# Splitting the first FFN products off r1 for one and a half feature tiles, and all squares for r2 on GpSimd

## The chip, the cores and the metric

The kernel runs on one core of a Trainium2 chip. The metric is the device time of one execution in microseconds (us), lower is better; it is given as the median of several runs. The engines are TensorE (PE, its weight loads are PEld), VectorE (DVE), ScalarE (ACT), GpSimd (POOL) and SyncE (SP), whose queue issues the weight loads.

## The reference

One layer of a streaming encoder, on 256 prompt rows and 64 sample rows (T = 320 columns in the kernel, which works on transposed data), model width 2048, feed-forward width 5632, all in float32:

```python
def layer(x, ...):
    h = rmsnorm(x, g_mix_pre)
    z = h @ w_in                      # pooling input u, and q, k, v
    ...                               # causal pooling mixer; chunk-banded attention with sinks
    mix = concat(pool_out, attn_out) @ w_out
    x = x + rmsnorm(mix, g_mix_post)              # r1 is the factor of this norm
    h = rmsnorm(x, g_ffn_pre)                     # r2 the factor of this one
    f = (silu(h @ w_gate) * (h @ w_up)) @ w_down
    return x + rmsnorm(f, g_ffn_post), ...
```

`rmsnorm(x, g)` is x times g divided by the root of the mean square over the 2048 features.

## The kernel before

The 2048 features lie in 16 tiles of 128 partitions (KT = 16), each with 320 columns. Every float32 matrix product is made of three matmuls on rounded halves: weights and data are split into a rounded part ("hi") and the rest ("lo"), and hi x hi, hi x lo and lo x hi are added in PSUM. ScalarE makes the hi part, VectorE the lo part (`lo` of a weight chunk, line 62; `scaled_split`, lines 120 to 122, for data). `chunk` loads 128x1024 weights into one of six raw buffers (two pools of three taken in turn) and splits them; hi and lo have three buffers each.

The change lies between the output projection and the first feed-forward products. There, `mix` holds the projection scaled by its gain and `x2` the input. r1 needs the sum of all squares of the projection, so it comes late. `rstd` (lines 103 to 118) sums squares over the partitions with a ones-matmul, and takes logarithm and exponential on ScalarE and four steps on VectorE.

The first four products (gate and up of the first two output tiles, 512 columns of weights in `wgu`) don't wait for r1 with all of their features. For the first AHEAD = 2 feature tiles, x2 and mix are multiplied by the weights apart: x2's products go into the four PSUM tiles `gu`, mix's into the four `qd`, from `pf`, which holds the split halves of both. They need no r1; `qd` is multiplied by r1 afterwards (`qr`, lines 622 and 625) and added to `gu` (line 627). These are 48 matmuls.

The residual loop (lines 559 to 573) goes over the feature tiles in the order 2 to 15, 0, 1. I call the place in that order the step n. For each step, `residual` makes t = mix x r1 on VectorE and adds it to x2, on VectorE for the first two steps and for even tiles, on GpSimd for odd tiles; it is called LEAD = 2 steps ahead. Then `scaled_split` writes the two halves of h2, ScalarE squares x2 into mix (line 568), and for the 14 tiles of the loop that weren't taken ahead twelve matmuls add to `gu`. Behind the loop, 14 squares are summed on GpSimd (line 577); the 15th tile's square and that sum go into two ones-matmuls for r2 (line 629). `gate_up(0)` and `gate_up(1)`, the next four products, run meanwhile; the first of them is `acc_g` at line 176.

Each engine executes its instructions in order. The order is made by a scheduler that places instructions by their dependencies, so it isn't always that of the code; `issue_after(ins)` ties the instructions in its block behind `ins`, if they are on the same engine as `ins`.

Of the kernel before, what the change touches and what calls it, by code (L numbers as in the profile page):

```python
# [12 lines left out]
F32R = mybir.dt.float32r  # L13
AF = mybir.ActivationFunctionType
ALU = mybir.AluOpType
# [6 lines left out]
P = 128  # L22
D = 2048
KT = D // P
NPR = 256
NSA = 64
T = NPR + NSA
# [5 lines left out]
NFF = FF // P  # L33
NH = NFF // 2
EPS = 1e-6
AHEAD = 2
LEAD = 2
WINS = (2, 4, 8, 16)


# [5 lines left out]
def trunk_kernel(ctx, tc, xT, wkv, wi, wo, wgu, wg, wu, wd, pw, par, ckT, cv, spT, yT, okT, ovT, ocv, ou):  # L46
    nc = tc.nc
# [19 lines left out]
    def chunk(src, kc, name, eng=nc.scalar):  # L67

        w = src.shape[2]
        n = kc * w  # L70
        pool, tag, bufs = raws[next(turn) % len(raws)]
        raw = pool.tile([P, 1024], F32, tag=tag, name=f"raw_{name}", bufs=bufs)
        nc.sync.dma_start(raw[:, :n].rearrange("p (k w) -> p k w", k=kc), src)
        hi, lo = split(raw, n, name, eng)
        return (hi[:, :n].rearrange("p (k w) -> p k w", k=kc),
                lo[:, :n].rearrange("p (k w) -> p k w", k=kc))
# [54 lines left out]
    def h1s(k):  # L131
        return h1[k // 4][:, 0, k % 4, :], h1[k // 4][:, 1, k % 4, :]
# [4 lines left out]
    for k0, n in ((0, 1), (1, 1)) + tuple((k, 2) for k in range(2, KT, 2)):  # L137
# [10 lines left out]
        wh, wl = chunk(wkv[:, k0 : k0 + n, :], n, f"kv{k0}", eng=nc.vector if k0 == 0 else nc.scalar)  # L148
        for k in range(k0, k0 + n):
            hh, hl = h1s(k)  # L150
            nc.vector.scalar_tensor_tensor(hl, x[:, k, :], col(C_PRE, k), hh.bitcast(F32),
                                           op0=ALU.mult, op1=ALU.subtract)
            for i, (ws, xs) in enumerate(((wh, hh), (wh, hl), (wl, hh))):
                for m in range(4):
                    nc.tensor.matmul(kv[m][:, :T], ws[:, k - k0, m * P : (m + 1) * P], xs,
                                     start=k == 0 and i == 0, stop=k == KT - 1 and i == 2)
# [108 lines left out]
    ks = at.tile([P, 2, T], F32, name="ks", tag="PT")  # L265
# [17 lines left out]
    for w in range(-1, 5):  # L283
        n = P if w < 4 else CH
# [190 lines left out]
    n = 3  # L475
# [23 lines left out]
    mix = big.tile([P, KT, T], F32, tag="C", name="mix")  # L499
# [17 lines left out]
    for m0 in range(0, KT, 2):  # L517
        between = ([*unit(11)[0], st_mm(1)], [st_mm(0)]) if m0 == 0 else ()

        def evac(i, a, m0=m0):  # L520
            m = m0 + i
            sq_acc(m, a[:, :T], acc1, "mix")
            nc.scalar.activation(mix[:, m, :], a[:, :T], AF.Copy, scale=col(C_POST, m))
        gemm([(wout(m), f"o{m}") for m in (m0, m0 + 1)], Ms, evac, between=between)
        if m0 == 0:
            actx.close()
            fctx = ctx.enter_context(tc.tile_pool(name="ff", bufs=1))
            raws += [(fctx, "wraw2", 3)]
        if m0 == 2:

            pf = fctx.tile([P, 2, 2, AHEAD, T], F32R, tag="A4", name="pf")
            for i, src in enumerate((x2, mix)):
                for k in range(AHEAD):
                    scaled_split(pf[:, i, 0, k, :], pf[:, i, 1, k, :], src[:, k, :], col(C_FPRE, k))
    ahead = chunk(wgu[:, 0:AHEAD, :], AHEAD, "gu0")
    r1 = rstd([acc1, last_sq.pop()], "1")


# [1 line left out]
    gu = [bank("ga"[m // 2], f"gu_{m}") for m in range(4)]  # L540
    qd = [bank("agga"[m], f"qd_{m}") for m in range(4)]
    wh, wl = ahead
    for i, accs in enumerate((gu, qd)):
        for m in range(4):
            sl = slice(m * P, m * P + P)
            for k in range(AHEAD):
                mm3(accs[m][:, :T], wh[:, k, sl], wl[:, k, sl], pf[:, i, 0, k, :], pf[:, i, 1, k, :],
                    k == 0, i == 1 and k == AHEAD - 1)
    qr = fctx.tile([P, 4, T], F32, tag="A5", name="qr")
    order = (*range(AHEAD, KT), *range(AHEAD))  # L550

    def residual(n):
        k = order[n]
        t = tmp320(f"t_{k}")
        nc.vector.tensor_tensor(t, mix[:, k, :], r1, op=ALU.mult)
        eng = nc.vector if n < 2 or k % 2 == 0 else nc.gpsimd
        return eng.tensor_tensor(x2[:, k, :], x2[:, k, :], t, op=ALU.add)

    for n in range(LEAD):
        residual(n)  # L560
    for n, k in enumerate(order):
        if n + LEAD < KT:
            added = residual(n + LEAD)
        if k >= AHEAD and k % 2 == 0:
            wh, wl = chunk(wgu[:, k : k + 2, :], 2, f"gu{k}")
        hh, hl = h2[k // 4][:, 0, k % 4, :], h2[k // 4][:, 1, k % 4, :]
        scaled_split(hh, hl, x2[:, k, :], col(C_FPRE, k))
        nc.scalar.activation(mix[:, k, :], x2[:, k, :], AF.Square)
        if k >= AHEAD:
            for i, (ws, xs) in enumerate(((wh, hh), (wl, hh), (wh, hl))):  # L570
                for m in range(4):
                    nc.tensor.matmul(gu[m][:, :T], ws[:, k % 2, m * P : m * P + P], xs, start=False,
                                     stop=i == 2 and k == KT - 1)

    with tc.issue_after(added.ins):
        for k in order[1:-1]:
            nc.gpsimd.tensor_tensor(mix[:, AHEAD, :], mix[:, AHEAD, :], mix[:, k, :], op=ALU.add)

    def h2s(k):
        return h2[k // 4][:, 0, k % 4, :], h2[k // 4][:, 1, k % 4, :]  # L580
# [8 lines left out]
    r2 = last_sig = None  # L589
    for half in range(2):  # L590
        s = [big.tile([P, 2, 4, T], F32R, tag=f"A{i}", name=f"s{half}_{i}") for i in range(4)]
        s += [fctx.tile([P, 2, 4, T], F32R, tag="A4", name=f"s{half}_4"),
              fctx.tile([P, 2, 2, T], F32R, tag="A5", name=f"s{half}_5")]

        def ss(k):
            return s[k // 4][:, 0, k % 4, :], s[k // 4][:, 1, k % 4, :]

        def evac_gu(n, ag, au):
            nm = f"{half}_{n}"
            g = tmp320(f"g_{nm}", "ev")  # L600
            uu = fctx.tile([P, T], F32, tag="ev2", name=f"u_{nm}", bufs=2)
            for i, (o, acc) in enumerate(((g, ag), (uu, au))):
                nc.vector.tensor_tensor(o, acc[:, :T], r2, op=ALU.mult)  # L603
            sg = fctx.tile([P, T], F32, tag="sg", name=f"sg_{nm}", bufs=2)
            nonlocal last_sig
            last_sig = nc.scalar.activation(sg, g, AF.Sigmoid)
            nc.gpsimd.tensor_tensor(g, g, uu, op=ALU.mult)  # L607
            nc.vector.tensor_tensor(g, g, sg, op=ALU.mult)
            sh, sl = ss(n)
            nc.scalar.copy(sh, g)  # L610
            nc.vector.tensor_tensor(sl, g, sh.bitcast(F32), op=ALU.subtract)

        def gate_up(b, lo_last=False):
            held = []
            gemm([(wgs(b), f"g{b}"), (wus(b), f"u{b}")], h2s, lambda i, a: held.append(a), tag="ga", lo_last=lo_last)
            return held

        n0 = 0
        if half == 0:

            for m in range(2):
                nc.vector.tensor_tensor(qr[:, m, :], qd[m][:, :T], r1, op=ALU.mult)
            held = gate_up(0, lo_last=True)
            for m in range(2, 4):
                nc.vector.tensor_tensor(qr[:, m, :], qd[m][:, :T], r1, op=ALU.mult)
            for m in range(4):
                nc.vector.tensor_tensor(qr[:, m, :], gu[m][:, :T], qr[:, m, :], op=ALU.add)
            held += gate_up(1)
            r2 = rstd([mix[:, order[-1], :], mix[:, AHEAD, :]], "2")
            evac_gu(0, qr[:, 0, :], qr[:, 1, :])  # L630
            evac_gu(1, qr[:, 2, :], qr[:, 3, :])
            evac_gu(2, *held[:2])
            evac_gu(3, *held[2:])
            n0 = 4
            f = big.tile([P, KT, T], F32, tag="C", name="f")
        for n in range(n0, NH):
            evac_gu(n, *gate_up(half * NH + n - 2))

        if half:
            with tc.issue_after(last_sig.ins):  # L640
                nc.scalar.preload_act_table_set(LNEXP)
        for m in range(KT):
            def evac(_, a, m=m):
                if m == KT - 1:
                    if half:
                        sq_acc(m, a[:, :T], acc3, "f")
                        nc.scalar.activation(f[:, m, :], a[:, :T], AF.Copy, scale=col(C_FPOST, m))
                elif half == 0:
                    nc.scalar.copy(f[:, m, :], a[:, :T])
                else:  # L650
                    nc.vector.tensor_tensor(f[:, m, :], f[:, m, :], a[:, :T], op=ALU.add)
                    sq_acc(m, f[:, m, :], acc3, "f")
                    nc.scalar.activation(f[:, m, :], f[:, m, :], AF.Copy, scale=col(C_FPOST, m))
            if m == KT - 1 and half == 0:
                held = bank("g", "acc_last")
            gemm([((lambda c, l, m=m: wd[half, m, :, c : c + l, :]), f"d{half}_{m}")], ss, evac, kt=NH,
                 tag="ag"[m % 2], accs=[held] if m == KT - 1 else None,
                 first=half == 0 or m < KT - 1, last=half == 1 or m < KT - 1)
# [8 lines left out]
    for k, n, how in TAIL:  # L667
# [7 lines left out]
        else:  # L675
            eng = nc.gpsimd if how == "g" else nc.vector
# [79 lines left out]
```

## Time and profile before

| | us |
|---|---|
| median of 3 runs | 1254.17 (1253.84 to 1254.76) |
| profiled execution | 1253.9 |
| its span, first to last instruction | 1252.1 |
| TensorE busy | 1238.6 (99%) |
| VectorE busy | 665.8 (53%) |
| ScalarE busy | 504.8 (40%) |
| GpSimd busy | 170.6 (14%) |

The rows come from the profiled execution; times in them are us from the start of its span, durations of one instruction in groups are ns. A row of the time list shows the start, the length, the engine, the line, the operation with the tile it writes and those it reads, the shape and the count of merged instructions, and in brackets how long the engine sat idle before it and what ended that. Instructions of an engine overlap at their ends, so the distance from one start to the next is what an instruction costs in a full queue. A released matmul is recorded with its full passage through the array, so its length is more than the distance to the next.

### The profile page before, as it was taken

Reading aid. Unit: us, or ns where it says so; the run is one execution under the profiler, and the core shown is the slowest. Engines: PE = TensorE matmul, PEld = TensorE weight load, DVE = VectorE, ACT = ScalarE, POOL = GpSimd, SP = SyncE. Lnnn points to the kernel's source line nnn. Section 1 sums busy time; section 2 is a strip of 40 time slices with the busy share of each in tenths; the row PEclk is TensorE's granted clock in tenths of the full one; section 3 lists DMA queues with packets and bytes.
Section 4 is the critical chain, followed back from the end, with each engine's and each line's share of the span. In section 5 each row is a group of like instructions: output and inputs, shape, how many; then the busy total and the mean of one; then the engine's idle time right before and its main releaser. Section 6 shows DMA issues by size and latency. Waiting matters only on the chain.

```text
span 1252.1 us, 20398 instructions
## 1 busy us (share of the span) xinstructions
PE 1238.6 (99%) x8404; PEld 1229.8 (98%) x8404; DVE 665.8 (53%) x889; ACT 504.8 (40%) x770; POOL 170.6 (14%) x153
## 2 busy tenths in 40 slices
PE   8999999999999999999999999999999999999997
PEld 8999999999999999999999999999999999999995
DVE  8867874336965455554433333554555455443435
ACT  5655654345543333333333333333333333443432
POOL 8202211122721000000000000000000000011112
PEclk9999999999999999999999999999999999999998
DMA  6654347443444444444455554444444444445532
GB/s 237 186 178 123 123 152 256 150 152 119 151 141 161 152 147 148 146 153 150 142 149 148 148 156 162 142 152 151 151 152 152 152 151 138 146 144 156 150 93 84
DMA packets 64125, 189.22 MB, mean 151 GB/s; under 512 B 15264, under 2 KB 16928, under 8 KB 64032
## 3 DMA queue, kind: packets, MB, share of 16 engines
q1 hardware_dynamic: 60480, 187.19, 46.1%
q8 instruction: 66, 1.08, 0.4%
q10 hardware_dynamic: 3552, 0.72, 0.3%
q14 instruction: 27, 0.22, 0.1%
HBM read 182.98 MB, written 3.27 MB: 149 GB/s over the span
## 4 chain that ended last, share of the span: by engine, by line
PE 93%; DVE 4%; issue 1%; DMA 1%; ACT 0%; POOL 0%; SPq 0%; DVEq 0%; ACTq 0%
PE acc_u L80 9%; PE acc_u L79 9%; PE acc_u L81 9%; PE acc_g L80 8%; PE acc_g L79 8%; PE acc_g L81 8%; PE acc_d L79 8%; PE acc_d L81 8%; PE acc_d L80 8%; PE acc_o L79 3%; PE acc_o L81 3%; PE acc_o L80 3%; PE acc_q L79 2%; PE acc_q L81 1%; PE acc_q L80 1%
## 5 line engine op out<-in xcount | busy, mean ns | idle before, releaser
L79 PE MATMUL acc_u<-h,hi_u 128*128 128x320 f32 x792 | 245.4, 310 | 0.0
L81 PE MATMUL acc_u<-h,lo_u 128*128 128x320 f32 x792 | 244.7, 309 | 0.0
L80 PE MATMUL acc_u<-h,hi_u 128*128 128x320 f32 x792 | 244.7, 309 | 0.0
L79 PE MATMUL acc_g<-h,hi_g 128*128 128x320 f32 x664 | 205.4, 309 | 0.0
L81 PE MATMUL acc_g<-h,lo_g 128*128 128x320 f32 x664 | 205.2, 309 | 0.0
L80 PE MATMUL acc_g<-h,hi_g 128*128 128x320 f32 x664 | 205.2, 309 | 0.0
L79 PE MATMUL acc_d<-s,hi_d 128*128 128x320 f32 x660 | 203.9, 309 | 0.0
L80 PE MATMUL acc_d<-s,hi_d 128*128 128x320 f32 x660 | 203.9, 309 | 0.0
L81 PE MATMUL acc_d<-s,lo_d 128*128 128x320 f32 x660 | 203.9, 309 | 0.0
L62 DVE TENSOR_TENSOR lo_d<-raw_d,hi_d 128x1024 fp32r<-128x1024 f32 (+1 forms) x96 | 110.3, 1149 | 175.6 <-ACT hi_d L60 175.6
L62 DVE TENSOR_TENSOR lo_g<-raw_g,hi_g 128x1024 fp32r<-128x1024 f32 x84 | 119.4, 1422 | 111.6 <-ACT hi_g L60 111.5
L60 ACT CAST hi_d<-raw_d 128x1024 fp32r<-128x1024 f32 (+1 forms) x96 | 93.8, 977 | 192.1 <-PE acc_d L80 179.3
L60 ACT CAST hi_g<-raw_g 128x1024 fp32r<-128x1024 f32 x84 | 88.3, 1051 | 180.7 <-PE acc_u L80 94.1
L60 ACT CAST hi_u<-raw_u 128x1024 fp32r<-128x1024 f32 x100 | 105.1, 1051 | 128.6 <-PE acc_g L80 102.9
L62 DVE TENSOR_TENSOR lo_u<-raw_u,hi_u 128x1024 fp32r<-128x1024 f32 x100 | 124.9, 1249 | 47.7 <-ACT hi_u L60 47.4
L79 PEld LDWEIGHTS acc_u<-h,hi_u 128*128 128x128 f32 x792 | 148.7, 188 | 0.0
L81 PEld LDWEIGHTS acc_u<-h,lo_u 128*128 128x128 f32 x792 | 148.7, 188 | 0.0
L80 PEld LDWEIGHTS acc_u<-h,hi_u 128*128 128x128 f32 x792 | 148.6, 188 | 0.0
L607 POOL TENSOR_TENSOR g<-g,u 128x320 f32<-128x320 f32 x44 | 41.5, 945 | 688.9 <-DVE u L603 665.6
L80 PEld LDWEIGHTS acc_g<-h,hi_g 128*128 128x128 f32 x664 | 124.7, 188 | 0.1
L79 PEld LDWEIGHTS acc_g<-h,hi_g 128*128 128x128 f32 x664 | 124.6, 188 | 0.1
L81 PEld LDWEIGHTS acc_g<-h,lo_g 128*128 128x128 f32 x664 | 124.6, 188 | 0.0
(210 smaller groups left out, 2018.1 us busy)
## 6 DMA issues: line engine op xcount, KB each, us to landing
raw_g<-wg SPq DMA_DIRECT2D x84, 512.0 KB, 3.6
raw_u<-wu SPq DMA_DIRECT2D x84, 512.0 KB, 3.6
raw_d<-wd SPq DMA_DIRECT2D x64, 512.0 KB, 3.5
raw_o<-wo SPq DMA_DIRECT2D x32, 512.0 KB, 3.8
raw_d<-wd SPq DMA_DIRECT2D x32, 384.0 KB, 3.4
raw_q<-wi SPq DMA_DIRECT2D x16, 512.0 KB, 3.9
raw_u<-wi SPq DMA_DIRECT2D x16, 512.0 KB, 3.7
raw_gu<-wgu SPq DMA_DIRECT2D x8, 512.0 KB, 3.5
```

The lines of the kernel that those rows point to most:

```text
L60: (eng.copy if eng is nc.scalar else eng.tensor_copy)(hi[:, :n], raw[:, :n])
L62: nc.vector.tensor_tensor(lo[:, :n], raw[:, :n], hi.bitcast(F32)[:, :n], op=ALU.subtract)
L79: nc.tensor.matmul(out, wh, xh, start=start, stop=False)
L80: nc.tensor.matmul(out, wh, xl, start=False, stop=False)
L81: nc.tensor.matmul(out, wl, xh, start=False, stop=stop)
L607: nc.gpsimd.tensor_tensor(g, g, uu, op=ALU.mult)
```

## The change

AHEAD becomes a pair. Feature tile 0 is still taken ahead in all four products, tile 1 only in the first two; its part of products 2 and 3 comes in the residual loop, with a weight chunk of its own (128x256). The order of the loop is now 2, 3, 4, 1, 5 to 15, 0. GpSimd makes the residual adds of the even steps from step 2 on, in place of those of the odd tiles; the last add, of step 15, is on VectorE. In the code, the first step's residual stands alone ahead of the loop, and the second's behind it. All 15 remaining squares are added into tile 2's on GpSimd, so that r2 needs one ones-matmul.

```diff
-AHEAD = 2
-LEAD = 2
+AHEAD = (4, 2)
+ORDER = (2, 3, 4, 1, *range(5, 16), 0)
...
-            for k in range(AHEAD):
+            n = sum(m < a for a in AHEAD)
+            for k in range(n):
                 mm3(accs[m][:, :T], wh[:, k, sl], wl[:, k, sl], pf[:, i, 0, k, :], pf[:, i, 1, k, :],
-                    k == 0, i == 1 and k == AHEAD - 1)
+                    k == 0, i == 1 and k == n - 1)
     qr = fctx.tile([P, 4, T], F32, tag="A5", name="qr")
-    order = (*range(AHEAD, KT), *range(AHEAD))
 
     def residual(n):
-        k = order[n]
+        k = ORDER[n]
         t = tmp320(f"t_{k}")
         nc.vector.tensor_tensor(t, mix[:, k, :], r1, op=ALU.mult)
-        eng = nc.vector if n < 2 or k % 2 == 0 else nc.gpsimd
+        eng = nc.vector if n < 2 or n % 2 else nc.gpsimd
         return eng.tensor_tensor(x2[:, k, :], x2[:, k, :], t, op=ALU.add)
 
-    for n in range(LEAD):
-        residual(n)
-    for n, k in enumerate(order):
-        if n + LEAD < KT:
-            added = residual(n + LEAD)
-        if k >= AHEAD and k % 2 == 0:
+    residual(0)
+    for n, k in enumerate(ORDER):
+        if n == 0:
+            residual(1)
+        if n + 2 < KT:
+            added = residual(n + 2)
+        m0 = AHEAD[k] if k < len(AHEAD) else 0
+        if m0 == 0 and k % 2 == 0:
             wh, wl = chunk(wgu[:, k : k + 2, :], 2, f"gu{k}")
+        ws, ks = (wh, wl), k % 2
+        if 0 < m0 < 4:
+            ws, ks = chunk(wgu[:, k : k + 1, m0 * P : 4 * P], 1, f"gu_{k}"), 0
...
-        if k >= AHEAD:
-            for i, (ws, xs) in enumerate(((wh, hh), (wl, hh), (wh, hl))):
-                for m in range(4):
-                    nc.tensor.matmul(gu[m][:, :T], ws[:, k % 2, m * P : m * P + P], xs, start=False,
-                                     stop=i == 2 and k == KT - 1)
+        for i, (w, xs) in enumerate(((ws[0], hh), (ws[1], hh), (ws[0], hl))):
+            for m in range(m0, 4):
+                o = (m - (m0 if 0 < m0 < 4 else 0)) * P
+                nc.tensor.matmul(gu[m][:, :T], w[:, ks, o : o + P], xs, start=False, stop=i == 2 and k == KT - 1)
 
     with tc.issue_after(added.ins):
-        for k in order[1:-1]:
-            nc.gpsimd.tensor_tensor(mix[:, AHEAD, :], mix[:, AHEAD, :], mix[:, k, :], op=ALU.add)
+        for k in ORDER[1:]:
+            nc.gpsimd.tensor_tensor(mix[:, ORDER[0], :], mix[:, ORDER[0], :], mix[:, k, :], op=ALU.add)
...
-            r2 = rstd([mix[:, order[-1], :], mix[:, AHEAD, :]], "2")
+            r2 = rstd([mix[:, ORDER[0], :]], "2")
```

GpSimd's queue from the last sum for r1 on, before the change (the number at the end of a `t` tile's name apart, the first number is the feature tile: `t_5` is tile 5's product with r1):

```order
L515 TENSOR_TENSOR acc1_2265<-acc1_2265,sq_mix_14_3357 128x320
L557 TENSOR_TENSOR x2_2259<-x2_2259,t_5_3473 128x320
L557 TENSOR_TENSOR x2_2259<-x2_2259,t_7_3515 128x320
L557 TENSOR_TENSOR x2_2259<-x2_2259,t_9_3557 128x320
L557 TENSOR_TENSOR x2_2259<-x2_2259,t_11_3599 128x320
L557 TENSOR_TENSOR x2_2259<-x2_2259,t_13_3641 128x320
L557 TENSOR_TENSOR x2_2259<-x2_2259,t_15_3683 128x320
L557 TENSOR_TENSOR x2_2259<-x2_2259,t_1_3725 128x320
L577 TENSOR_TENSOR mix_2264<-mix_2264 128x320 x14
```

All seven residual adds stand ahead of the 14 sums of squares. The same queue after the change:

```order
L515 TENSOR_TENSOR acc1_2265<-acc1_2265,sq_mix_14_3357 128x320
L557 TENSOR_TENSOR x2_2259<-x2_2259,t_4_3437 128x320
L581 TENSOR_TENSOR mix_2264<-mix_2264 128x320 x2
L557 TENSOR_TENSOR x2_2259<-x2_2259,t_5_3479 128x320
L581 TENSOR_TENSOR mix_2264<-mix_2264 128x320 x2
L557 TENSOR_TENSOR x2_2259<-x2_2259,t_7_3521 128x320
L581 TENSOR_TENSOR mix_2264<-mix_2264 128x320 x2
L557 TENSOR_TENSOR x2_2259<-x2_2259,t_9_3563 128x320
```

The adds and the sums now alternate, one add and two sums, and go on so up to the add of tile 15, behind which three sums stand.

VectorE's queue at the end of the residual loop, before the change (`h2_3` holds the halves of tiles 12 to 15, `h2_0` those of tiles 0 to 3):

```order
L62 TENSOR_TENSOR lo_gu14_3708<-raw_gu14_3704,hi_gu14_3706 128x1024
L557 TENSOR_TENSOR x2_2259<-x2_2259,t_0_3701 128x320
L122 SCALAR_TENSOR_TENSOR h2_3_3385<-x2_2259,pr_71,h2_3_3385 128x320
L555 TENSOR_TENSOR t_1_3725<-mix_2264,r_1_3380 128x320
L122 SCALAR_TENSOR_TENSOR h2_3_3385<-x2_2259,pr_71,h2_3_3385 128x320
L122 SCALAR_TENSOR_TENSOR h2_0_3382<-x2_2259,pr_71,h2_0_3382 128x320
L622 TENSOR_TENSOR qr_3442<-qd_0_3390,r_1_3380 128x320
L622 TENSOR_TENSOR qr_3442<-qd_1_3391,r_1_3380 128x320
L122 SCALAR_TENSOR_TENSOR h2_0_3382<-x2_2259,pr_71,h2_0_3382 128x320
L62 TENSOR_TENSOR lo_g0_0_3778<-raw_g0_0_3774,hi_g0_0_3776 128x1024
```

The split of tile 1 is the `h2_0` row behind the two `qr`. After the change:

```order
L62 TENSOR_TENSOR lo_gu14_3714<-raw_gu14_3710,hi_gu14_3712 128x1024
L557 TENSOR_TENSOR x2_2259<-x2_2259,t_0_3707 128x320
L122 SCALAR_TENSOR_TENSOR h2_3_3385<-x2_2259,pr_71,h2_3_3385 128x320 x2
L122 SCALAR_TENSOR_TENSOR h2_0_3382<-x2_2259,pr_71,h2_0_3382 128x320
L626 TENSOR_TENSOR qr_3430<-qd_0_3390,r_1_3380 128x320
L626 TENSOR_TENSOR qr_3430<-qd_1_3391,r_1_3380 128x320
L62 TENSOR_TENSOR lo_g0_0_3779<-raw_g0_0_3775,hi_g0_0_3777 128x1024
```

All splits, tile 1's at step 3 among them, now stand ahead of `qr`.

## Rows read from the trace of the kernel before

**Rows 1.** The page's first part: busy us, share of the span, instructions of each engine.

```profile
PE 1238.6 (99%) x8404; PEld 1229.8 (98%) x8404; DVE 665.8 (53%) x889; ACT 504.8 (40%) x770; POOL 170.6 (14%) x153
```

**Rows 2.** Stretches: from:to, length, busy us of PE, PEld, DVE, ACT, POOL; clock, DMA.

```profile
10.00:20.00 10.00, 7.93 (x51) 7.41 (x52) 10.00 (x7) 6.63 (x12) 9.94 (x9) 1.00 0.68 238
...
305.00:330.00 25.00, 24.75 (x168) 24.26 (x166) 24.92 (x40) 17.61 (x35) 13.36 (x9) 1.00 0.31 106
330.00:345.00 15.00, 15.00 (x103) 15.00 (x103) 11.94 (x13) 5.51 (x6) 14.22 (x11) 1.00 0.59 187
...
1240.00:1252.00 12.00, 6.33 (x12) 3.87 (x12) 7.90 (x9) 2.56 (x6) 3.42 (x2) 0.64 0.55 205
```

**Rows 3.** Time list, TensorE, at the loop's start and behind its end.

```profile
304.65 0.75 PE L572 MATMUL gu<-h,hi_gu 128*128 128x320 f32 x4
305.24 0.75 PE L572 MATMUL gu<-h,lo_gu 128*128 128x320 f32 x4
...
329.96 2.58 PE L176 MATMUL acc_g<-h,hi_g 128*128 128x320 f32 x16 [0.23 <-DVE qr L622]
```

**Rows 4.** Time list, VectorE, from r1 to the loop's end.

```profile
301.50 0.90 DVE L555 TENSOR_TENSOR t<-mix,r 128x320 f32<-128x320 f32 x2
302.31 0.89 DVE L557 TENSOR_TENSOR x<-x,t 128x320 f32<-128x320 f32 x2
303.11 0.48 DVE L555 TENSOR_TENSOR t<-mix,r 128x320 f32<-128x320 f32 x1
303.52 0.55 DVE L122 SCALAR_TENSOR_TENSOR h<-x,pr,h 128x320 fp32r<-128x320 f32 x1
303.98 0.48 DVE L557 TENSOR_TENSOR x<-x,t 128x320 f32<-128x320 f32 x1
...
308.01 1.17 DVE L555 TENSOR_TENSOR t<-mix,r 128x320 f32<-128x320 f32 x1
309.11 1.21 DVE L62 TENSOR_TENSOR lo_gu<-raw_gu,hi_gu 128x1024 fp32r<-128x1024 f32 x1
310.24 0.48 DVE L557 TENSOR_TENSOR x<-x,t 128x320 f32<-128x320 f32 x1
...
328.94 0.88 DVE L622 TENSOR_TENSOR qr<-qd,r 128x320 f32<-128x320 f32 x2
329.74 0.54 DVE L122 SCALAR_TENSOR_TENSOR h<-x,pr,h 128x320 fp32r<-128x320 f32 x1
```

**Rows 5.** Groups by shape, VectorE, 300 to 330 us: count, busy us, mean ns.

```profile
L122 DVE SCALAR_TENSOR_TENSOR h<-x,pr,h 128x320 fp32r<-128x320 f32 x16 | 11.1, 699 | 0.0
L555 DVE TENSOR_TENSOR t<-mix,r 128x320 f32<-128x320 f32 x16 | 9.7, 611 | 0.0
```

**Rows 6.** Time list, GpSimd: two residual adds and the sums of squares.

```profile
307.71 1.13 POOL L557 TENSOR_TENSOR x<-x,t 128x320 f32<-128x320 f32 x1 [1.24 <-DVE t L555]
311.67 3.06 POOL L557 TENSOR_TENSOR x<-x,t 128x320 f32<-128x320 f32 x1 [2.83 <-DVE t L555]
...
328.63 20.03 POOL L577 TENSOR_TENSOR mix<-mix 128x320 f32<-128x320 f32 x14
```

**Rows 7.** Time list at the kernel's head, VectorE, then GpSimd.

```profile
30.41 1.63 DVE L62 TENSOR_TENSOR lo_kv<-raw_kv,hi_kv 128x1024 fp32r<-128x1024 f32 x1
...
34.24 1.62 DVE L62 TENSOR_TENSOR lo_kv<-raw_kv,hi_kv 128x1024 fp32r<-128x1024 f32 x1
...
29.99 0.97 POOL L145 TENSOR_TENSOR sqx<-x 128x320 f32<-128x320 f32 x1
31.03 2.82 POOL L147 TENSOR_TENSOR acc<-acc,sqx 128x320 f32<-128x320 f32 x2
```

**Rows 8.** Groups by shape, VectorE, 330 to 341 us: the weight splits.

```profile
L62 DVE TENSOR_TENSOR lo_g<-raw_g,hi_g 128x1024 fp32r<-128x1024 f32 x3 | 5.0, 1683 | 0.0
L62 DVE TENSOR_TENSOR lo_u<-raw_u,hi_u 128x1024 fp32r<-128x1024 f32 x2 | 3.1, 1556 | 0.0
```

**Rows 9.** Time list, TensorE: the ones-matmuls for r2.

```profile
358.20 1.24 PE L107 MATMUL ss<-mix,ones 128*128 128x320 f32 x4
```

More of the change, by code (lines that the diff above doesn't have):

```diff
@@ L529, in trunk_kernel @@
         if m0 == 2:
-            pf = fctx.tile([P, 2, 2, AHEAD, T], F32R, tag="A4", name="pf")
+            pf = fctx.tile([P, 2, 2, len(AHEAD), T], F32R, tag="A4", name="pf")
             for i, src in enumerate((x2, mix)):
-                for k in range(AHEAD):
+                for k in range(len(AHEAD)):
                     scaled_split(pf[:, i, 0, k, :], pf[:, i, 1, k, :], src[:, k, :], col(C_FPRE, k))
-    ahead = chunk(wgu[:, 0:AHEAD, :], AHEAD, "gu0")
+    ahead = chunk(wgu[:, 0:2, :], 2, "gu0")
     r1 = rstd([acc1, last_sq.pop()], "1")
@@ L545, in trunk_kernel @@
             sl = slice(m * P, m * P + P)
-            for k in range(AHEAD):
+            n = sum(m < a for a in AHEAD)
+            for k in range(n):
                 mm3(accs[m][:, :T], wh[:, k, sl], wl[:, k, sl], pf[:, i, 0, k, :], pf[:, i, 1, k, :],
-                    k == 0, i == 1 and k == AHEAD - 1)
+                    k == 0, i == 1 and k == n - 1)
     qr = fctx.tile([P, 4, T], F32, tag="A5", name="qr")
-    order = (*range(AHEAD, KT), *range(AHEAD))
     def residual(n):
-        k = order[n]
+        k = ORDER[n]
         t = tmp320(f"t_{k}")
         nc.vector.tensor_tensor(t, mix[:, k, :], r1, op=ALU.mult)
-        eng = nc.vector if n < 2 or k % 2 == 0 else nc.gpsimd
+        eng = nc.vector if n < 2 or n % 2 else nc.gpsimd
         return eng.tensor_tensor(x2[:, k, :], x2[:, k, :], t, op=ALU.add)
-    for n in range(LEAD):
-        residual(n)
-    for n, k in enumerate(order):
-        if n + LEAD < KT:
-            added = residual(n + LEAD)
-        if k >= AHEAD and k % 2 == 0:
+    residual(0)
[6 more added lines that the diff above has]
+        if m0 == 0 and k % 2 == 0:
             wh, wl = chunk(wgu[:, k : k + 2, :], 2, f"gu{k}")
+        ws, ks = (wh, wl), k % 2
+        if 0 < m0 < 4:
+            ws, ks = chunk(wgu[:, k : k + 1, m0 * P : 4 * P], 1, f"gu_{k}"), 0
         hh, hl = h2[k // 4][:, 0, k % 4, :], h2[k // 4][:, 1, k % 4, :]
```

## The prediction

> **What bounds the kernel now.** I read the page's first part, then the stretch table, then engine by engine the list of instructions between 296 and 345 us, where the diff is. TensorE is busy 99% of the span [rows 1], so time can come only from fewer matmuls or from a wait that TensorE feels. In the table [rows 2] the stretch from 305 to 330 us is special: TensorE is busy for 24.75 of 25 us, and VectorE for 24.92. Elsewhere VectorE has room (11.94 of 15 us behind it). So in the residual loop two engines are full at once, and TensorE is fed just in time: the first product behind the loop waits for VectorE's `qr` [rows 3].
>
> How far VectorE is full can be read off its list [rows 4]: from 301.50, when r1 is there, to the last h2 split (starts 329.74, 0.46 long) it runs 28.70 us without a gap. Undisturbed, an instruction takes 0.40 us from its start to the next one's (`t`: 303.11 to 303.52; residual add the same, 302.31 to 303.11 for two), an h2 split 0.46 (303.52 to 303.98), a weight split 1.13 (309.11 to 310.24).
>
> Some take much longer: the `t` at 308.01 needs 1.17 us, and the next starts 1.10 later, so 0.69 are lost. In the group rows [rows 5] the 16 splits have a mean of 699 ns and the 16 `t` one of 611, where undisturbed ones take some 545 and 480; (699-545)x16 + (611-480)x16 = 4.6 us, or 0.65 for each of the seven GpSimd adds of the loop. They fall where those run: GpSimd's add runs from 307.71 for 1.13 us [rows 6], across the start of that `t`. A GpSimd add costs VectorE 0.65 us here, although the two touch different tiles.
>
> **What the change moves in the order.** This is the point on which I forecast. In the kernel before, GpSimd's 14 sums of squares start after its last residual add, at 328.63 [rows 6], since `issue_after(added.ins)` ties them to it. In the changed kernel the last `added` (step 15, odd) is a VectorE instruction, and the built order has no such tie any more: two sums stand behind each of the first six residual adds on GpSimd's queue, three behind the seventh. 12 sums now stand ahead of the seventh add, thus in the loop in which VectorE has no room.
>
> The price of a sum comes from two places. The loop's own adds cost 0.65 each. At the kernel's head the same mix has run already [rows 7]: VectorE's period from 30.41 to 34.24 us is 3.83 long, for one weight split and two h splits that take 1.13 + 2x0.46 = 2.05 undisturbed. GpSimd ran three operations in one period (one from 29.99, two from 31.03 for 2.82 us), so each cost (3.83-2.05)/3 = 0.59. I take 0.64, nearer to the loop's own row since the loop has its instructions: 12 x 0.64 = 7.7 us. Lower bound: from 330 to 341 us, the next stretch with sums, VectorE's five weight splits took 3 x 1.68 + 2 x 1.56 = 8.2 us [rows 8] where undisturbed ones take 5 x 1.21, so 2.1 were lost to the 11/1.43 = 7.7 sums that fit (14 in 20.03 us [rows 6]), 0.27 each; there six of VectorE's twelve operations read PSUM. That gives 12 x 0.27 = 3.3. A gain is excluded: moving sums ahead frees VectorE behind 330 us, where TensorE has no idle time to give back (15.00 of 15 us [rows 2]).
>
> The Trainium skill ("SBUF — State Buffer", SBUF: two separate sides) says that VectorE with two SBUF inputs and GpSimd share one port pair, held for a whole instruction, while the other blocks. The shortest GpSimd operation shown took 0.97 us [rows 7]; if a full one were lost each time, 12 would cost 11.6 us, and the sum below would end at 1266.4. The trace shows the blocking, but at 0.65 rather than 0.97, so I stay with the rows.
>
> **The rest, part by part.** *Products.* Ahead of r1, 12 matmuls go; 6 come back in the loop (feature tile 1, products 2 and 3). At 0.147 us each (four in 304.65 to 305.24 [rows 3]), TensorE has 6 x 0.147 = 0.88 us less to do, but its stock of work that needs no r1 ends 1.76 us earlier, at 302.9, ahead of the first h2 split (303.52 on VectorE). It waits there some 0.6 us. Neither shows in the end if VectorE sets the pace.
>
> *VectorE.* Feature tile 1 moves from the end, where it ran behind `qr` (329.74), to step 3, so VectorE must have finished all but the last two splits before the loop's last but one tile is multiplied. One quarter-width weight split is new: between 0.30 (a quarter of 1.21) and 0.40 (any 320-column operation), I take 0.35. VectorE's work up to the split of step 13 is then 28.70, less `qr` (0.80 from 328.94 to 329.74 [rows 4]) and two splits (0.92), plus 0.35: 27.33 us, so without any sums it ends at 328.8. Residual adds stay nine on VectorE, seven on GpSimd.
>
> *TensorE's end of the loop.* Behind that split it still has four matmuls of step 13 and twelve of step 14: 16 x 0.147 = 2.35, plus about 0.1 for the handoff, so 331.3. The two `qr` on VectorE finish 1.72 us behind the split and are covered. Against 329.96 this is +1.3 us, with no sum priced.
>
> *r2.* One ones-matmul goes: four records for two matmuls take 1.24 us [rows 9], so -0.62, on TensorE's path with no wait. GpSimd needs one sum more, but r2's matmul comes at 358.20 and the sums ended at 348.7 (328.63 + 20.03 [rows 6]), and now end earlier; cover is 9 us.
>
> *The new DMA* (128 KB), its ScalarE cast and the shifted buffers: SyncE's queue, past which it moves every later load by one place, loads as far ahead as six buffers allow; the loop takes a chunk in two steps, so five chunks ahead are still most of the loop. The cast is a quarter-width one on ScalarE, busy for 17.61 of 25 us [rows 2]. I cost both at nothing; with the cover gone, the quarter-width chunk would come late once, and delay two of four products of one tile (0.88 us of matmuls).
>
> *First tile's residual first.* In the built order VectorE's two first `t` and two first adds stand as before (t, t, x, x, t, h), so this edit does nothing.
>
> **The new wait.** The add of an even step n+2 now stands on GpSimd's queue behind the sum of step n, which waits for ScalarE's square of n. Behind the add wait ScalarE's h2 cast, VectorE's split and TensorE. A pair of steps on VectorE takes 9 operations, 2x0.40 + 0.40 + 2x0.46 + 1.13 = 3.25, plus three GpSimd operations at 0.64: 5.2 us. GpSimd's three take 1.13 + 2x1.43 (20.03/14 [rows 6]) = 4.0 us. It keeps pace, with 1.2 us for the handoffs.
>
> **Sum.** +1.3 (loop end without sums) + 7.7 (12 sums) - 0.6 (r2) = +8.4 us. The profiled execution took 1253.9, which would become 1262.3; it lies 0.27 below the median of the runs, so against 1254.17 I predict **1262.5 us**.
>
> **Rivals.**
> *A. The sums are free* (the other side). GpSimd slips them into moments when VectorE waits or reads PSUM, and waits itself, as in the add of 3.06 us at 311.67 [rows 6]. Then +1.3 - 0.6 = +0.7, 1254.9; if VectorE's deadline also eased so that the 0.88 is kept, 1253. It decides when a sum costs under 0.15 us, (2.5-0.7)/12. Against it: the 4.6 us lost in the loop [rows 5] make 0.65 for each add only if that one cost VectorE its share too, and VectorE has no waits in the loop. 8%.
> *B. GpSimd becomes the bound.* With an add at 3.06 in each pair, its three take 3.06 + 2x1.43 = 5.9 us against 5.2; over six pairs +4.5 us more: 1267. Against it: the add at 307.71 took 1.13, and so did most. 8%.
> *C. TensorE's clock falls,* as its work comes in bursts with waits. 174 matmuls of 0.147 (25.6 us) would be spread over some 36 us, 71%. At the head, 51 matmuls lay in the 10 us from 10 to 20, 75% by the same count, and the clock granted was 1.00; it was 0.64 only in the last 12 us, with 12 matmuls [rows 2]. At half clock TensorE would need 51 us, +15 us: 1277. 3%. The Trainium skill ("TensorE: Matmul & The Clock Gate", HAM oscillation — how this bites in real kernels) warns of waits between bursts; the head's row speaks against it here.
>
> **Chances and range.** Forecast with its bounds 81%, A 8%, B 8%, C 3%. With the lower bound of 0.27 for a sum it is 4.4 less, 1258.1; B gives 1267. Range 1258 to 1267. A measurement of this kernel can tell about 0.2%, 2.5 us. Slower by more: forecast, B and C, 91% (some of the first left out for cheap sums). Within: 7%. Faster by more: 2% for what I haven't seen, since all savings in sight (0.88 + 0.62 + the wait of 0.23 [rows 3]) stay below 2.5.
>
> **What would show it.** GpSimd's list with sums between the residual adds from about 305 us on; some 19 instead of 7 stretched VectorE operations and a loop mean for `t` and h2 splits up by 0.2 us or more; the first product behind the loop at about 339 instead of 329.96; TensorE busy some 71% in the loop with a granted clock of 1.00; two r2 records instead of four. I'm wrong if VectorE's instructions beside the sums keep 0.48 and 0.55 us, if GpSimd falls far behind, or if TensorE runs through the loop without idle time.

## The result and the profile after

| | before | after |
|---|---|---|
| median of the runs, us | 1254.17 (1253.84 to 1254.76) | 1265.3 (1264.52 to 1265.41) |
| ratio | | 1.0088, 95% interval 1.0075 to 1.01 |
| profiled execution, us | 1253.9 | 1265.21 |
| its span, us | 1252.1 | 1263.1 |

The changed kernel is 11.1 us slower. 1262.5 was predicted, with a range of 1258 to 1267. The page of the changed kernel, first part:

```profile
PE 1239.1 (98%) x8396; PEld 1227.7 (97%) x8396; DVE 672.5 (53%) x890; ACT 505.8 (40%) x771; POOL 166.2 (13%) x154
```

Against [rows 1], TensorE is busy for as long as before (1239.1 against 1238.6 us) in a span that is 11 us longer: it waited. The stretch table shows where (columns as in [rows 2]):

```profile
305.00:330.00 25.00, 18.97 (x115) 16.77 (x116) 25.00 (x31) 14.24 (x28) 18.88 (x16) 1.00 0.23 82
330.00:345.00 15.00, 12.45 (x80) 11.40 (x79) 15.00 (x21) 7.67 (x13) 8.57 (x7) 1.00 0.30 96
```

In [rows 2] TensorE was busy for 24.75 us of the 25 from 305 to 330. Now it is 18.97, and 12.45 of the next 15. VectorE has no idle moment in either, and the clock stays at 1.00, which of TensorE's two levels is the full one. TensorE's time list gives the loop's first matmul, two waits of one pair of steps, and the first product behind the loop:

```profile
304.83 0.85 PE L577 MATMUL gu<-h,hi_gu 128*128 128x320 f32 x4 [0.39 <-ACT h L121]
...
317.04 0.85 PE L577 MATMUL gu<-h,lo_gu 128*128 128x320 f32 x4 [0.87 <-DVE lo_gu L62]
318.58 1.43 PE L577 MATMUL gu<-h,hi_gu 128*128 128x320 f32 x8 [0.70 <-DVE h L122]
...
342.30 2.51 PE L176 MATMUL acc_g<-h,hi_g 128*128 128x320 f32 x16
```

Behind 314 us the same two waits recur in every pair of steps, one for the weight split (`lo_gu`), one for the h2 split, both of VectorE. What VectorE did in one pair, from its time list, with the loop's first and last rows:

```profile
302.89 0.90 DVE L555 TENSOR_TENSOR t<-mix,r 128x320 f32<-128x320 f32 x2
...
314.00 1.16 DVE L555 TENSOR_TENSOR t<-mix,r 128x320 f32<-128x320 f32 x1
315.09 1.90 DVE L62 TENSOR_TENSOR lo_gu<-raw_gu,hi_gu 128x1024 fp32r<-128x1024 f32 x1
316.91 1.16 DVE L557 TENSOR_TENSOR x<-x,t 128x320 f32<-128x320 f32 x1
317.99 0.54 DVE L122 SCALAR_TENSOR_TENSOR h<-x,pr,h 128x320 fp32r<-128x320 f32 x1
318.45 0.48 DVE L555 TENSOR_TENSOR t<-mix,r 128x320 f32<-128x320 f32 x1
318.85 0.54 DVE L122 SCALAR_TENSOR_TENSOR h<-x,pr,h 128x320 fp32r<-128x320 f32 x1
319.31 1.17 DVE L555 TENSOR_TENSOR t<-mix,r 128x320 f32<-128x320 f32 x1
...
339.26 1.46 DVE L122 SCALAR_TENSOR_TENSOR h<-x,pr,h 128x320 fp32r<-128x320 f32 x3
340.64 0.88 DVE L626 TENSOR_TENSOR qr<-qd,r 128x320 f32<-128x320 f32 x2
```

And GpSimd's list over the same pair, with the two sums that end within the loop last:

```profile
313.69 1.12 POOL L557 TENSOR_TENSOR x<-x,t 128x320 f32<-128x320 f32 x1 [1.29 <-DVE t L555]
314.77 2.94 POOL L581 TENSOR_TENSOR mix<-mix 128x320 f32<-128x320 f32 x2
319.01 1.12 POOL L557 TENSOR_TENSOR x<-x,t 128x320 f32<-128x320 f32 x1 [1.29 <-DVE t L555]
...
336.04 2.95 POOL L581 TENSOR_TENSOR mix<-mix 128x320 f32<-128x320 f32 x2
```

One pair of steps took 319.31 - 314.00 = 5.31 us. In the kernel before it took 3.93, half of the 7.85 us from GpSimd's add at 307.71 [rows 6] to the next but one:

```profile
315.56 1.13 POOL L557 TENSOR_TENSOR x<-x,t 128x320 f32<-128x320 f32 x1 [0.83 <-DVE t L555]
```

Three of VectorE's instructions are stretched, `t`, the weight split and the residual add, and each begins while one of the three GpSimd operations runs: the add from 313.69, the sums from 314.77. A weight split took 1.21 us in [rows 4] and takes 1.90 here, the residual add 0.48 and 1.16. Each loses about the same, 0.68 or 0.69.

Since the start of the loop varies by up to 3 us between profiled executions (it is 301.50 before, 302.89 here, and up to 304.39 below), I compare loop lengths: from the start of the first `t` to the start of `acc_g`. Before it is 329.96 - 301.50 = 28.46 us [rows 3, 4], after 342.30 - 302.89 = 39.41, or +10.95. The r2 matmul saves its part: two records instead of the four of [rows 9]. The rows are the first product behind the ones-matmuls before, and the ones-matmul and that product after:

```profile
359.03 0.55 PE L79 MATMUL acc_g<-h,hi_g 128*128 128x320 f32 x1
...
370.46 0.70 PE L107 MATMUL ss<-mix,ones 128*128 128x320 f32 x2
370.76 0.55 PE L79 MATMUL acc_g<-h,hi_g 128*128 128x320 f32 x1
```

From the start of `acc_g` to there it was 359.03 - 329.96 = 29.07 us and is 370.76 - 342.30 = 28.46, so 0.61 are saved on TensorE's path. 10.95 - 0.61 = 10.3 of the measured 11.1 are thereby placed. The other 0.8 is not: in the two profiled executions the loop starts 1.39 us later after the change, and what follows that product is 0.7 shorter, so the stretches outside vary by about as much.

### The profile page after: what moved, and what is told of

It reads as the page before. It is cut to its first block, busy times and chain, and to the rows that moved or that the text cites. A ratio compares the mean times of both kernels' runs of the same rounds, so it can differ in the third digit from the quotient of the medians.

```text
span 1263.1 us, 20388 instructions
## 1 busy us (share of the span) xinstructions
PE 1239.1 (98%) x8396; PEld 1227.7 (97%) x8396; DVE 672.5 (53%) x890; ACT 505.8 (40%) x771; POOL 166.2 (13%) x154
## 4 chain that ended last, share of the span: by engine, by line
PE 93%; DVE 5%; issue 1%; DMA 1%; ACT 0%; SPq 0%; DVEq 0%; ACTq 0%
PE acc_u L79 9%; PE acc_u L81 9%; PE acc_u L80 9%; PE acc_g L79 8%; PE acc_g L81 8%; PE acc_g L80 8%; PE acc_d L81 8%; PE acc_d L80 8%; PE acc_d L79 8%; PE acc_o L81 3%; PE acc_o L79 3%; PE acc_o L80 3%; PE acc_q L80 1%; PE acc_q L79 1%; PE acc_q L81 1%
```

## The experiments

Theory: each GpSimd sum in the residual loop takes 0.69 us from VectorE, which has none to spare. Rivals: P, the products taken less far ahead cost the time; W, the residual adds wait in GpSimd's queue behind the sums; F, a sum costs a fixed time of handing over, whatever its length. "Length" is the loop length as above, from each kernel's own trace; the last column is the kernel before as measured in the same round.

| kernel | length, us | median, us | beside it, before |
|---|---|---|---|
| before | 28.46 | 1254.17 | |
| after | 39.41 | 1265.3 | 1254.17 |
| b_free | 37.19 | 1262.94 | 1254.36 |
| a_dveadds | 37.46 | 1262.84 | 1254.36 |
| a_half | 34.43 | 1259.21 | 1254.36 |
| a_tied | 31.27 | 1256.81 | 1254.3 |
| a_dve_late | 27.96 | 1253.41 | 1254.3 |
| b_r2one | 28.45 | 1254.07 | 1254.3 |
| b_dve_late | 27.81 | 1252.9 | 1254.3 |

### The kernel before, with the tie taken off: b_free

```diff
-    with tc.issue_after(added.ins):
-        for k in order[1:-1]:
-            nc.gpsimd.tensor_tensor(mix[:, AHEAD, :], mix[:, AHEAD, :], mix[:, k, :], op=ALU.add)
+    for k in order[1:-1]:
+        nc.gpsimd.tensor_tensor(mix[:, AHEAD, :], mix[:, AHEAD, :], mix[:, k, :], op=ALU.add)
```

> The kernel before, without the tie of the sums of squares to the last residual add, and nothing else changed. GpSimd's queue then alternates between one residual add and two sums. Theory (each GpSimd sum that runs in the residual loop takes 0.69 us from VectorE, which has no slack there): 13 sums stand ahead of the last residual add, 13 x 0.69 = 9.0, so 1254.2 + 9.0 = 1263.2, plus or minus 1, with VectorE still without idle time. Rival P (it is the products taken less far ahead and the new place of feature tile 1 that cost): 1254.2, no change.

Measured: ratio 1.0067 (1.0052 to 1.0082), +8.6 us. The loop is 8.73 longer, against 13 x 0.69 = 8.97. The groups by shape of VectorE from 300 to 342 us (count, busy us, mean ns, idle):

```profile
L555 DVE TENSOR_TENSOR t<-mix,r 128x320 f32<-128x320 f32 x16 | 11.7, 737 | 0.0
L122 DVE SCALAR_TENSOR_TENSOR h<-x,pr,h 128x320 fp32r<-128x320 f32 x16 | 10.4, 657 | 0.0
L62 DVE TENSOR_TENSOR lo_gu<-raw_gu,hi_gu 128x1024 fp32r<-128x1024 f32 x5 | 9.5, 1902 | 0.0
L557 DVE TENSOR_TENSOR x<-x,t 128x320 f32<-128x320 f32 x9 | 8.3, 933 | 0.0
```

All five weight splits of the loop are stretched (1902 ns where [rows 4] had 1.21 us). No product and no feature tile was moved in this kernel, so rival P isn't needed for the bulk of the loss: the missing tie alone makes it.

### The changed kernel, with the tie restored: a_tied

```diff
+    added = None
     for n, k in enumerate(ORDER):
...
         if n + 2 < KT:
-            added = residual(n + 2)
+            got = residual(n + 2)
+            added = added if (n + 2) % 2 else got
```

> The changed kernel with the sums of squares tied to the last residual add on GpSimd (step 14), so that all 15 stand behind it in the queue; nothing else changed. Theory (of the 11.1 us, 14 sums at 0.69 are 9.7; the rest is the later loop end by 1.3, less 0.6 for r2): 1265.3 - 9.7 = 1255.6; by the prediction's own terms 1254.9. Range 1254.4 to 1256. Rival P (the products and the new place of feature tile 1 cost most of it): 1263 to 1265.

Measured: 1256.81, ratio 1.0019 (1.0011 to 1.0028): 8.5 of the 11.1 us are gone, and 2.5 stay, more than the 0.7 to 1.4 I had given. The loop is 31.27 long, 2.81 more than before. VectorE's list at its end, GpSimd's, and TensorE's first product behind it:

```profile
302.08 0.89 DVE L555 TENSOR_TENSOR t<-mix,r 128x320 f32<-128x320 f32 x2
...
328.12 1.16 DVE L122 SCALAR_TENSOR_TENSOR h<-x,pr,h 128x320 fp32r<-128x320 f32 x1
329.56 0.81 DVE L122 SCALAR_TENSOR_TENSOR h<-x,pr,h 128x320 fp32r<-128x320 f32 x1 [0.28 <-ACT h L121]
331.32 1.08 DVE L122 SCALAR_TENSOR_TENSOR h<-x,pr,h 128x320 fp32r<-128x320 f32 x1 [0.96 <-ACT h L121]
332.33 0.88 DVE L628 TENSOR_TENSOR qr<-qd,r 128x320 f32<-128x320 f32 x2
```

```profile
325.87 3.06 POOL L557 TENSOR_TENSOR x<-x,t 128x320 f32<-128x320 f32 x1 [2.83 <-DVE t L555]
328.90 20.10 POOL L583 TENSOR_TENSOR mix<-mix 128x320 f32<-128x320 f32 x15
```

```profile
333.35 1.84 PE L176 MATMUL acc_g<-h,hi_g 128*128 128x320 f32 x11 [1.41 <-DVE qr L628]
```

The seventh add was sent at 325.87 and took 3.06 us, as one of the two in [rows 6] did. ScalarE's cast of that step waits for it, with a weight cast behind it on its queue:

```profile
328.97 0.56 ACT L121 ACTIVATE h<-x,pr 128x320 fp32r<-128x320 f32 x1 [3.08 <-POOL x L557]
...
329.79 1.03 ACT L60 CAST hi_g<-raw_g 128x1024 fp32r<-128x1024 f32 x1
```

The splits on VectorE (329.56 and 331.32, with gaps ahead of them, and themselves lengthened beside the sums that start at 328.90) and `qr` come late behind that, and TensorE waits 1.41 us for `qr`. In the kernel before, GpSimd's last add belonged to tile 1, whose h2 halves no product of the loop reads, so a late add at this place could hold up nothing in it. So this wait, 1.4 of the 2.8 us, goes by the trace with the new order of tiles; after the change, with the sums in the loop, `acc_g` has no such wait. The other 1.4 is near the later loop end that was priced at 1.3.

### All residual adds on VectorE, sums free: a_dveadds

```diff
-        eng = nc.vector if n < 2 or n % 2 else nc.gpsimd
-        return eng.tensor_tensor(x2[:, k, :], x2[:, k, :], t, op=ALU.add)
+        return nc.vector.tensor_tensor(x2[:, k, :], x2[:, k, :], t, op=ALU.add)
```

> The changed kernel with all 16 residual adds on VectorE; the 15 sums run on GpSimd as their squares come. No residual add can wait behind a sum any more. Theory (the sums cost by slowing VectorE's instructions, 0.69 each): 14 sums still cost 9.7; the seven adds cost VectorE 0.40 each instead of 0.69, -2.0; 1265.3 - 2.0 = 1263.3, plus or minus 1. Rival W (the adds wait in GpSimd's queue behind the sums, and that costs): the whole cost of the sums goes, 1255 or less.

Measured: 1262.84, +8.5 us. Nothing that TensorE waits for stands on GpSimd's queue here, and the loss is there all the same, so rival W falls. The groups of VectorE from 300 to 342 us:

```profile
L556 DVE TENSOR_TENSOR x<-x,t 128x320 f32<-128x320 f32 x16 | 15.8, 992 | 0.0
L122 DVE SCALAR_TENSOR_TENSOR h<-x,pr,h 128x320 fp32r<-128x320 f32 x16 | 9.1, 579 | 0.0
L555 DVE TENSOR_TENSOR t<-mix,r 128x320 f32<-128x320 f32 x16 | 8.3, 523 | 0.0
L62 DVE TENSOR_TENSOR lo_gu<-raw_gu,hi_gu 128x1024 fp32r<-128x1024 f32 x5 | 6.1, 1212 | 0.0
```

GpSimd's sums now strike mostly residual adds (992 ns in the mean, 0.48 us undisturbed), for the weight splits keep 1212 ns. Against the next kernel but one, a_dve_late, which differs only by the sums' place, the loop is 37.46 - 27.96 = 9.50 longer: 14 sums at 0.68.

### Sums of half the width: a_half

```diff
         for k in ORDER[1:]:
-            nc.gpsimd.tensor_tensor(mix[:, ORDER[0], :], mix[:, ORDER[0], :], mix[:, k, :], op=ALU.add)
+            nc.gpsimd.tensor_tensor(mix[:, ORDER[0], : T // 2], mix[:, ORDER[0], : T // 2], mix[:, k, : T // 2],
+                                    op=ALU.add)
```

> The changed kernel with sums of squares over 160 of 320 columns (the other half of the sum is left out), at the same places in the queue. Theory (VectorE is held for as long as GpSimd's instruction works on its data): the 0.69 of a sum becomes about half, 14 x 0.35 = 4.8 less, 1260.5, plus or minus 1. Rival F (each sum costs a fixed time of handing over, whatever its length): 1265.3.

Measured: 1259.21, which is 1.3 below the 1260.5 expected and just outside the plus or minus 1. The loop is what was expected: 39.41 - 34.43 = 4.98 us shorter than after, against 14 x 0.35 = 4.9. Of the rest, 0.72 is in the profiled executions the start of the loop (302.17 here, 302.89 after). VectorE's time list, the pair of steps that answers to the one above:

```profile
311.79 1.16 DVE L555 TENSOR_TENSOR t<-mix,r 128x320 f32<-128x320 f32 x1
312.88 1.55 DVE L62 TENSOR_TENSOR lo_gu<-raw_gu,hi_gu 128x1024 fp32r<-128x1024 f32 x1
314.35 0.81 DVE L557 TENSOR_TENSOR x<-x,t 128x320 f32<-128x320 f32 x1
```

The `t` still meets a full-width residual add and takes 1.16; the weight split and the residual add meet sums of half the width and take 1.55 and 0.81, that is 0.34 and 0.33 more than undisturbed. Half the columns, half the loss: rival F falls. At these two widths VectorE loses some 2.15 ns for each of GpSimd's columns.

### All residual adds on VectorE, sums behind the loop: a_dve_late and b_dve_late

In both, the sums are added into the square of the loop's last tile, which doesn't exist before the loop ends. a_dve_late is the changed kernel with this:

```diff
-        eng = nc.vector if n < 2 or n % 2 else nc.gpsimd
-        return eng.tensor_tensor(x2[:, k, :], x2[:, k, :], t, op=ALU.add)
+        return nc.vector.tensor_tensor(x2[:, k, :], x2[:, k, :], t, op=ALU.add)
...
-    with tc.issue_after(added.ins):
-        for k in ORDER[1:]:
-            nc.gpsimd.tensor_tensor(mix[:, ORDER[0], :], mix[:, ORDER[0], :], mix[:, k, :], op=ALU.add)
+    last = ORDER[-1]
+    for k in ORDER[:-1]:
+        nc.gpsimd.tensor_tensor(mix[:, last, :], mix[:, last, :], mix[:, k, :], op=ALU.add)
...
-            r2 = rstd([mix[:, ORDER[0], :]], "2")
+            r2 = rstd([mix[:, ORDER[-1], :]], "2")
```

> The changed kernel with all residual adds on VectorE, and the sums added into the square of the loop's last tile, so that none can start before the loop has ended. Theory: no sum and no add on GpSimd slows VectorE in the loop; seven adds cost 0.40 instead of 0.69, -2.0 of VectorE's work against the tied form; TensorE then sets the loop's end, some 0.7 ahead of the kernel before, and r2 saves 0.6: 1252.9, range 1252.3 to 1253.7. Rival (adds on GpSimd relieve VectorE, since they take 0.40 us of work from it): slower than the tied form, 1255.5 to 1257.

b_dve_late makes the same two edits in the kernel before, with its own order of tiles and all 48 products ahead.

> The kernel before, with one ones-matmul for r2, the sums behind the loop, and all residual adds on VectorE. Theory: VectorE's loop gets 2.0 us shorter, TensorE no longer waits in it (0.7 us in the kernel before), and r2 saves 0.6: 1252.9, range 1252.3 to 1253.5, the same as with fewer products taken ahead. Rival (as above): 1255 or more.

Measured: a_dve_late 1253.41, ratio 0.9993 (0.9984 to 1.0002), not to be told from the kernel before; b_dve_late 1252.9, ratio 0.9989 (0.998 to 0.9998), the lowest of all, with an interval that ends just below 1. The groups of VectorE in b_dve_late from 300 to 342 us, and its first product behind the loop:

```profile
L122 DVE SCALAR_TENSOR_TENSOR h<-x,pr,h 128x320 fp32r<-128x320 f32 x16 | 8.7, 545 | 0.0
L555 DVE TENSOR_TENSOR t<-mix,r 128x320 f32<-128x320 f32 x16 | 7.7, 485 | 0.0
L556 DVE TENSOR_TENSOR x<-x,t 128x320 f32<-128x320 f32 x16 | 7.7, 484 | 0.0
```

```profile
332.20 2.51 PE L176 MATMUL acc_g<-h,hi_g 128*128 128x320 f32 x16
```

No group is stretched (545, 485 and 484 ns, and 1220 for the weight splits), and TensorE hardly waits: from the first `t` at 304.39 the loop is 332.20 - 304.39 = 27.81, against 28.46 before. The kernel of the next section, b_r2one, differs from b_dve_late only by the seven adds on GpSimd: its loop is 28.45 - 27.81 = 0.64 longer, and its median 1.2 higher (the other half of that is a wait shown there). An add that GpSimd takes over costs VectorE 0.65 in the mean [rows 5], where VectorE's own add takes 0.40; the seven adds were dearer on GpSimd than they are on VectorE. That the loop gains 0.64 and not 7 x 0.25 is because TensorE now sets its length. With fewer products taken ahead, a_dve_late is no shorter (27.96): its 0.88 us of saved matmuls go into a wait of 0.4 for ScalarE's first h2 and some smaller ones.

### The kernel before, with one ones-matmul for r2: b_r2one

```diff
-    with tc.issue_after(added.ins):
-        for k in order[1:-1]:
-            nc.gpsimd.tensor_tensor(mix[:, AHEAD, :], mix[:, AHEAD, :], mix[:, k, :], op=ALU.add)
+    last = order[-1]
+    for k in order[:-1]:
+        nc.gpsimd.tensor_tensor(mix[:, last, :], mix[:, last, :], mix[:, k, :], op=ALU.add)
...
-            r2 = rstd([mix[:, order[-1], :], mix[:, AHEAD, :]], "2")
+            r2 = rstd([mix[:, order[-1], :]], "2")
```

> The kernel before, with all squares for r2 added into that of the loop's last tile on GpSimd, behind the loop, and one ones-matmul for r2 instead of two. Theory: only the matmul goes, -0.6: 1253.6. Rival (r2 comes later since GpSimd has one sum more, and TensorE waits for it): 1254.2 or more.

Measured: 1254.07 against 1254.3, ratio 0.9998 (0.9989 to 1.0007). The interval holds both -0.6 and nothing, so the times don't settle it. Its trace shows two r2 records instead of four, a loop of the same length, and no wait of TensorE for r2. But it shows another wait, behind the loop. The rows are VectorE's last h2 split and TensorE's fourth matmul of `acc_g`, whose first starts at 330.71:

```profile
330.49 1.19 DVE L122 SCALAR_TENSOR_TENSOR h<-x,pr,h 128x320 fp32r<-128x320 f32 x1
...
331.73 2.17 PE L176 MATMUL acc_g<-h,hi_g 128*128 128x320 f32 x13 [0.34 <-DVE h L122]
```

GpSimd's first sum starts at 330.45, with that split, which takes 1.19 instead of the 0.54 of [rows 4], and TensorE needs its result: the fourth matmul starts 331.73 - (330.71 + 3 x 0.147) = 0.58 late. From `acc_g` to the product behind the ones-matmul (359.84) it is 29.13 us, where it was 29.07 before. So the saved matmul was paid away by one sum at the wrong moment, by the trace the same effect once more; in the changed kernel the saving came through (28.46).

## Why the prediction was right

**The order decides.** That the tie doesn't reach an engine other than that of its instruction, and that the sums therefore come into the loop, was the step on which the forecast rested. b_free makes that edit alone and loses 8.6 of the 11.1 us; a_tied takes it back and regains 8.5.

**The price of a sum, 12 x 0.64 = 7.7.** Both factors were low. The trace has 14 sums slowing VectorE in the loop, not 12: GpSimd kept pace so well that two of the three sums behind the seventh add still fell into it (at 336.04, the last row of GpSimd's list above). And each costs 0.69, the loss of a single stretched instruction in [rows 4], not 0.64; I had let the 0.59 of the kernel's head [rows 7] draw it down. The 0.65 of [rows 5] was itself a mean over two kinds: a struck h2 split loses less (1.16 against 0.54 in a_tied, at 328.12), and after the change all but one of the struck instructions are of the dearer kinds. 14 x 0.69 = 9.66. This term makes 2.0 of the 2.8 us by which the forecast was low; the other 0.8 is the part that isn't placed. The lower bound of 0.27 was a mean too: of the five weight splits in that stretch three took 1.90 us, so lost the same 0.69, and two took 1.21 and 1.26. In the loop no sum came off free.

**The loop's end without sums, +1.3.** In the changed kernel 10.95 - 9.66 = 1.29, as worked out: VectorE's split at 339.26 ends at 339.72, and `acc_g` starts 2.58 us behind it (2.45 was given for 16 matmuls and the handoff). Where the sums are gone from the loop, in a_tied, it is 2.8, for the reason shown there: the prediction had the two `qr` covered by 1.72 us, and there they are not. So rival A's time of 1254.9 was 2 us too low.

**First tile, new load, r2.** TensorE waits 0.39 us at the loop's start (0.6 was given), for ScalarE's cast of the first h2. The quarter-width split takes 0.41 us undisturbed in a_tied, 0.33 to the next start (0.35 given). No engine waits for the new load. The first `t` and adds stand in the old order. The r2 matmul's 0.62 came out as 0.61.

**What was to be seen.** The first product behind the loop came at 342.30, not at about 339: the loop was 2.0 longer than forecast, and started 1.4 later. TensorE was busy for 76% of the time from 305 to 330 (71% was given). The sums stood between the adds, and 21 VectorE instructions were stretched, where 19 were expected: the groups of the changed kernel from 300 to 342 us are

```profile
L555 DVE TENSOR_TENSOR t<-mix,r 128x320 f32<-128x320 f32 x16 | 12.4, 781 | 0.0
L62 DVE TENSOR_TENSOR lo_gu<-raw_gu,hi_gu 128x1024 fp32r<-128x1024 f32 x6 | 10.7, 1789 | 2.3 <-ACT hi_gu L60 2.3
L122 DVE SCALAR_TENSOR_TENSOR h<-x,pr,h 128x320 fp32r<-128x320 f32 x16 | 9.1, 580 | 0.0
L557 DVE TENSOR_TENSOR x<-x,t 128x320 f32<-128x320 f32 x9 | 9.0, 1007 | 0.0
...
L62 DVE TENSOR_TENSOR lo_gu<-raw_gu,hi_gu 128x256 fp32r<-128x256 f32 x1 | 1.1, 1079 | 0.0
```

The sixth weight split, and its 2.3 us of idle time, lie ahead of r1. Against undisturbed means of 484, 1212, 545, 480 and 414 ns that makes 4.75 + 3.46 + 0.56 + 4.74 + 0.67 = 14.2 us, or 0.68 for each of 7 adds and 14 sums. I had named `t` and the h2 splits as those whose mean would rise. `t` rose by 170 ns, but the h2 splits fell from 699 [rows 5] to 580; residual adds and weight splits were struck in their place. The price was sized from a total, and came out near (0.64 against 0.69); which instruction meets GpSimd's follows from the order of the moment.

**The rivals.** B didn't come: from the pair at 313.69 on GpSimd idled 1.29 us in each waiting for `t`, and its adds took 1.12 us, all but the first. A pair came out at 5.31 us, where 5.2 was given; the prediction calls VectorE's part of it nine operations, but its sum of 3.25, and the list above, have six. C didn't come: with 115 matmuls in 25 us the granted clock stayed at 1.00. The Trainium skill's rule ("SBUF — State Buffer", SBUF: two separate sides) would have given 1266.4, closer to the time than my sum, but by luck: with the 14 sums that ran it would have been 1268.4 (14 x 0.97). VectorE lost 0.69 us beside an add that is recorded with 1.12, and 0.34 at half the width. A recorded length can hold a wait of GpSimd's own, as the 3.06 in [rows 6] suggests, so it can't be taken for the price.

## What to carry to other kernels

Where VectorE is full, an elementwise operation on GpSimd isn't free: here it cost VectorE 0.6 to 0.7 us for 320 float32 columns, more than the 0.40 that VectorE takes for the same add itself. So look, before work is moved to GpSimd, at whether VectorE feeds the bound engine at that moment, and put what can wait behind that stretch by a dependency in the data (here, adding into the tile that is ready last), since a tie in the order ends without notice when its anchor moves to another engine. When a change of a rule picks other engines for instructions, read the built order for everything that was anchored to them.

## What I had not expected of the hardware

GpSimd doesn't take the same time for the same add. In the kernel before an add sent into VectorE's full queue took 1.13 us at 307.71 and 3.06 at 311.67 [rows 6]; in a_tied three of seven took 3.06, though they were sent at the same place of VectorE's sequence. With the sums between, all but the first took 1.12. VectorE's loss was nearly the same: 0.69 on the `t` beside a short one ([rows 4], 308.01), 0.62 on the h2 split beside a long one (a_tied, 328.12). What makes GpSimd take longer was not tried, and stays open.
